# Attention-head operations of VectorE and ScalarE given a higher scheduling priority in a two-layer decoder trunk

## The chip, the cores and the metric

The kernel runs on one core of a Trainium2 chip. The metric is the device time in microseconds (us) of one execution. Lower is better.

The core has five engines that matter here. TensorE (PE in the profile) multiplies matrices; its weight loads are listed apart as PEld. VectorE is DVE, ScalarE is ACT, GpSimd is POOL, and SyncE (SP) issues the weight DMAs. Each engine has its own list of instructions, whose order is fixed when the program is built.

## The reference

A decoder trunk of two layers works on 256 tokens of width 2048, all in float32. Layer 0 normalises the tokens, projects them, and sends three quarters of the columns through a pooling mixer and one quarter through a 4-head attention over 256 memory rows. Layer 1 projects into queries for 12 differential heads and again 4 memory heads. Each layer ends in an output projection and a squared-ReLU MLP. What the change touches is the heads:

```python
# one differential head (layer 1), for two query/key maps
a = probs(q1b, k1) - lam * probs(q2b, k2)      # softmax of masked scores
o = jnp.einsum('bhqk,bkhd->bqhd', a, v)
token_out = rms_norm(o, subln_norm[b]) * (1.0 - lam_init)
# one memory head (both layers)
s = jnp.einsum('bqhd,bkhd->bhqk', q, k) * (MEM_HEAD_DIM ** -0.5)
o = jnp.einsum('bhqk,bkhd->bqhd', jax.nn.softmax(s, axis=-1), v)
```

## The kernel before, in words

**Weights.** All weights stream from one packed tensor `in_w` into SBUF as float32. TensorE works on a shorter float form, so each weight block is split in two: ScalarE rounds it into a high part (`hi_ring`, L157) and VectorE subtracts that from the original to get the low part (`lo_ring`, L158). A product is then high x high, high x low and low x high. This is the "making of high and low parts". Both parts live in a ring of six slots of 512 columns (`SLOTS`, L27). A unit of four 128-column blocks is called a quad here; it fills one slot. `Feed.fill` (L196) is called ahead of the matmuls of a quad and traces the splits up to three quads beyond it (`AHEAD`, L27). For some quads of the MLP's second matrix (the "slab" jobs) VectorE first forms sums of raw weights (L181 to L184).

**Projections.** `b_tile` (L423) computes a 256 x 512 tile in 16 steps of one quad and six matmuls (L417 to L419). `c_tile` (L400) computes 128 output columns in 16 blocks (L405 to L407). `a_part` (L377) does the same with a wide moving side (L391, L393). All of them call `tick()` once per quad.

**Heads.** The heads are woven between the quads. `at(d, fn)` (L280) puts a step of a head on a list, and `tick` (L283) traces it `d` quads later. A differential head (`diff_head`, L1175) has four steps. `scores` multiplies queries and keys on TensorE, adds the mask on VectorE (L1202, L1203; for heads 8 to 11 TensorE adds it), takes maxima (L1207), lets ScalarE exponentiate (L1211) and combines the two maps on VectorE (L1217 to L1221). `turn` transposes on TensorE (L1226) and copies on ScalarE (L1227). `pv` multiplies with the values (L1232 to L1234), takes squares on ScalarE (L1242) and scales on VectorE (L1250). `back` transposes (L1255) and writes high and low parts of the result into `cat1` (`split_gain`, L368). A memory head is `mem_query` (L541) and `mem_head` (L566), with the same kind of steps. `turn_queries` (L1155) transposes the queries and copies them on ScalarE (L1163). `query_rows`, `rope` and `query_scale` (L474 to L516) prepare the queries of four heads. The result tiles of all heads feed the output projection `out_tiles` (L1028), whose first three tiles need the last heads.

**What sets the order.** The program is traced in Python order, and each instruction's priority is its place in that order. When the program is built, a scheduler plays it through and puts, on each engine, the instruction with the best priority among those whose inputs and buffers it reckons to be ready. The result is a fixed list for each engine, which the chip runs in that order. In the kernel before, a step of a head that is traced at some tick stands ahead of the splits that are traced after that tick, and behind those traced before.

**Buffers around the change.** PSUM tiles: tag `s` (two), `t`, `o` and `st` (one each). SBUF tiles: tag `v` (six of 256 columns: `mq`, `mq_sq`, `osb`, `o_sq` and others), `m2` (twelve small columns).

Of the kernel before, what the change touches and what calls it, by code (L numbers as in the profile page):

```python
# [10 lines left out]
F32 = mybir.dt.float32  # L11
F32R = mybir.dt.float32r
BF16 = mybir.dt.bfloat16
AF = mybir.ActivationFunctionType
ALU = mybir.AluOpType
# [3 lines left out]
P = 128  # L19
# [243 lines left out]
def program(ctx, tc, plan, dry, xT, memT, par, lam, cst, wst, yT):  # L263
# [26 lines left out]
            tick()  # L290


    def vt(name):
        return tp.tile([P, T], F32, tag="v", bufs=6, name=name)

# [245 lines left out]
    def mem_query(src, gq, cols):  # L541


        q = vt("mq")
        sq = vt("mq_sq")
        nc.scalar.activation(q, src, AF.Copy, scale=gq)
        nc.scalar.activation(sq, src, AF.Square)
        y = tp.tile([P, 2], F32, tag="m2", bufs=12, name="mq_y")

        def stats():  # L550
            st = stat("st_mq")
            for t in range(2):
                nc.tensor.matmul(
                    st[:, 2 * t : 2 * t + 2], sq[:, t * P : t * P + P], ones_h,
                    start=True, stop=True,
                )
            v2 = tp.tile([P, 2], F32, tag="m2", bufs=12, name="mq_v")
            nc.vector.tensor_mul(v2, st[:, 0:4].rearrange("p (a b) -> p a b", b=2)[:, :, 0], cols[1])
            nc.vector.tensor_scalar_add(v2, v2, EPS)
            rsqrt_cols(y, v2)  # L560
            nc.vector.tensor_mul(y, y, cols[0])

        at(2, stats)
        return q, y

    def mem_head(q, y, k, v, e, pT, out, lag, pv_lag=6):  # L566

        def scores():  # L570
            s = pp.tile([P, 2, T], F32, tag="s", bufs=2, name="ms")
            for t in range(2):
                nc.tensor.matmul(s[:, t, :], q[:, t * P : t * P + P], k, start=True, stop=True)
            m = tp.tile([P, 2], F32, tag="m2", bufs=12, name="mm_max")
            nc.vector.tensor_reduce(out=m, in_=s, axis=AX.X, op=ALU.max, negate=True)
            nc.vector.tensor_mul(m, m, y)
            z = tp.tile([P, 2], F32, tag="m2", bufs=12, name="mm_sum")
            for t in range(2):
                nc.scalar.activation(
                    e[:, t, :], s[:, t, :], AF.Exp, bias=m[:, t : t + 1], scale=y[:, t : t + 1],  # L580
                    accum_out=z[:, t : t + 1],
                )
            zr = tp.tile([P, 2], F32, tag="m2", bufs=12, name="mm_rec")
            nc.vector.reciprocal(zr, z)
            for t in range(2):
                nc.vector.tensor_scalar_mul(e[:, t, :], e[:, t, :], zr[:, t : t + 1])

        def turn():
            t4 = pp.tile([P, 2, T], F32, tag="t", bufs=1, name="mt")
            for mb in range(2):  # L590
                for t in range(2):
                    nc.tensor.transpose(
                        t4[:, mb, t * P : t * P + P], e[:, t, mb * P : mb * P + P], ident
                    )
            nc.scalar.copy(pT, t4)

        def pv():
            o = pp.tile([P, T], F32, tag="o", bufs=1, name="mo")
            for mb in range(2):
                nc.tensor.matmul(o, v(mb), pT[:, mb, :], start=mb == 0, stop=mb == 1)  # L600
            nc.scalar.copy(out[:, 0:T], o)
            nc.vector.tensor_sub(out[:, T : 2 * T], o, out[:, 0:T].bitcast(F32))

        at(lag, scores)
        at(lag + 4, turn)
        at(lag + pv_lag, pv)
# [548 lines left out]
    def turn_queries(rows, i, pair):  # L1155
        t4 = pp.tile([P, 2, T], F32, tag="t", bufs=1, name="tq")
        for c in range(2):
            for t in range(2):
                nc.tensor.transpose(
                    t4[:, c, t * P : t * P + P], rows[:, t, (i + c) * P : (i + c) * P + P], ident  # L1160
                )
        for g, r in enumerate((slice(0, 64), slice(64, 128))):
            nc.scalar.activation(pair[g][r], t4[r], AF.Copy, scale=qcol[r])  # L1163


    gsub = cp.tile([P, 1], F32, name="gsub")
# [8 lines left out]
    def diff_head(h, q, y, lag, pv_lag, back_lag, by_pe):  # L1175
# [6 lines left out]
        def scores():  # L1182
            s1 = pp.tile([P, 2, T], F32, tag="s", bufs=2, name="s1")
            s0 = pp.tile([P, 2, P], F32, tag="s", bufs=2, name="s0")
            if by_pe:
                for m in range(2):
                    kk = kT[:, 6 * m + j, :]
                    nc.tensor.matmul(s1[:, m, :], q[:, m, P:T], kk, start=True, stop=False)
                    nc.tensor.matmul(s1[:, m, P:T], idb, mkb, start=False, stop=True)
                for m in range(2):  # L1190
                    kk = kT[:, 6 * m + j, 0:P]
                    nc.tensor.matmul(s0[:, m, :], q[:, m, 0:P], kk, start=True, stop=False)
                    nc.tensor.matmul(s0[:, m, :], idb, mkb, start=False, stop=True)
            else:
                for m in range(2):
                    kk = kT[:, 6 * m + j, :]
                    nc.tensor.matmul(s1[:, m, :], q[:, m, P:T], kk, start=True, stop=True)
                for m in range(2):
                    kk = kT[:, 6 * m + j, 0:P]
                    nc.tensor.matmul(s0[:, m, :], q[:, m, 0:P], kk, start=True, stop=True)  # L1200
                mask = const[:, C_MASK : C_MASK + P].unsqueeze(1).to_broadcast([P, 2, P])
                nc.vector.tensor_add(s1[:, :, P:T], s1[:, :, P:T], mask)  # L1202
                nc.vector.tensor_add(s0, s0, mask)  # L1203
            mx = tp.tile([P, 2, 2], F32, tag="m4", bufs=6, name="mx")
            z = tp.tile([P, 2, 2], F32, tag="m4", bufs=6, name="z")
            for t, s in ((1, s1), (0, s0)):
                nc.vector.tensor_reduce(out=mx[:, t, :], in_=s, axis=AX.X, op=ALU.max, negate=True)  # L1207
            nc.vector.tensor_mul(mx, mx, yh)
            for t, s, e in ((1, s1, e1), (0, s0, e0)):
                for m in range(2):  # L1210
                    nc.scalar.activation(  # L1211
                        e[:, m, :], s[:, m, :], AF.Exp, bias=mx[:, t, m : m + 1],
                        scale=yh[:, t, m : m + 1], accum_out=z[:, t, m : m + 1],
                    )

            zr = tp.tile([P, 2], F32, tag="m2", bufs=12, name="zr")
            nc.vector.reciprocal(zr, z[:, :, 1])  # L1217
            stt(zr, zr, nlam, z[:, :, 0], ALU.mult, ALU.mult)
            stt(ez, z[:, :, 0], EPS, z[:, :, 0], ALU.mult, ALU.mult)
            for t, e, dst in ((1, e1, a[:, P : P + T]), (0, e0, a[:, 0:P])):  # L1220
                stt(dst, e[:, 1, :], zr[:, t : t + 1], e[:, 0, :], ALU.mult, ALU.add)  # L1221

        def turn():
            t3 = pp.tile([P, 384], F32, tag="t", bufs=1, name="dt")
            for i in range(3):
                nc.tensor.transpose(t3[:, i * P : i * P + P], a[:, i * P : i * P + P], ident)  # L1226
            nc.scalar.copy(aT, t3)  # L1227

        def pv():
            o = pp.tile([P, 2, P], F32, tag="o", bufs=1, name="do")  # L1230
# [1 line left out]
            nc.tensor.matmul(o[:, 0, :], aT[:, 0:P], vv[:, 0, hs], start=True, stop=True)  # L1232
            nc.tensor.matmul(o[:, 1, :], aT[:, P:T], vv[:, 0, hs], start=True, stop=False)
            nc.tensor.matmul(o[:, 1, :], aT[:, T : T + P], vv[:, 1, hs], start=False, stop=True)  # L1234
            osb = vt("osb").rearrange("p (a b) -> p a b", a=2)
            if by_pe:
                nc.vector.tensor_copy(osb, o)
                o = osb
            ss = tp.tile([P, 2], F32, tag="m2", bufs=12, name="o_ss")
            junk = vt("o_sq")  # L1240
            for t in range(2):
                nc.scalar.activation(  # L1242
                    junk[:, t * P : t * P + P], o[:, t, :], AF.Square, accum_out=ss[:, t : t + 1]
                )
            v = tp.tile([P, 2], F32, tag="m2", bufs=12, name="o_v")
            stt(v, ss, 1.0 / P, ez, ALU.mult, ALU.add)
            yo = tp.tile([P, 2], F32, tag="m2", bufs=12, name="o_y")
            rsqrt_cols(yo, v)
            for t in range(2):
                nc.vector.tensor_scalar_mul(osb[:, t, :], o[:, t, :], yo[:, t : t + 1])  # L1250

            def back():
                f = pp.tile([P, T], F32, tag="st", bufs=1, name="o_t")
                for t in range(2):
                    nc.tensor.transpose(f[:, t * P : t * P + P], osb[:, t, :], ident)  # L1255
                split_gain(cat1[:, h, :], f, gsub)

            at(back_lag, back)

# [4 lines left out]
    for c in range(3):  # L1264
        ps = pair_of_banks(0, "q1")
        b_tile(ps, "w_in_q", 1, c, x_mx)
        rows, v = query_rows(ps, c1, 64)
        rope(rows, qtab)
        y = query_scale(v, c1)
        for i in range(2):  # L1270
            j = 2 * c + i
            q = qb[j % 3]
# [104 lines left out]
```

## Time and profile before

| what | value |
|---|---|
| median of 3 runs | 2045.28 us (2045.19 to 2045.52) |
| the profiled execution | 2044.93 us |
| its span, first to last instruction | 2043.1 us |
| granted TensorE clock | 1.000 of full speed |

How to read the profile. A row of the windows view gives, for a stretch in us from the start of the span, its length and then for each engine the busy time and the number of instructions, followed by the granted clock, the share of the DMA engines and the DMA rate. A row of the waits view names an engine and its instruction (by the tile that it writes and its line), what released it, and the total, the count and the longest of those waits. A row of the timeline gives start, duration, engine, line, operation, tiles written and read, shapes and a count; idle time just before it stands in square brackets. TensorE's matmuls overlap in the records: each is shown longer than the distance to the next one's start.

The heads of layer 0 run between about 60 and 130 us, those of layer 1 between about 1150 and 1280 us.

### The profile page before, as it was taken

Reading aid. Unit: us, or ns where it says so; the run is one execution under the profiler, and the core shown is the slowest. Engines: PE = TensorE matmul, PEld = TensorE weight load, DVE = VectorE, ACT = ScalarE, POOL = GpSimd, SP = SyncE. Lnnn points to the kernel's source line nnn. Section 1 sums busy time; section 2 is a strip of 40 time slices with the busy share of each in tenths; the row PEclk is TensorE's granted clock in tenths of the full one; section 3 lists DMA queues with packets and bytes.
Section 4 is the critical chain, followed back from the end, with each engine's and each line's share of the span. In section 5 each row is a group of like instructions: output and inputs, shape, how many; then the busy total and the mean of one; then the engine's idle time right before and its main releaser. Section 6 shows DMA issues by size and latency. Waiting matters only on the chain.

```text
span 2043.1 us, 32257 instructions
## 1 busy us (share of the span) xinstructions
PE 2037.2 (100%) x11060; PEld 1755.3 (86%) x11060; DVE 1716.2 (84%) x3215; ACT 1349.8 (66%) x2505; POOL 51.9 (3%) x67
## 2 busy tenths in 40 slices
PE   9999999999999999999999999999999999999999
PEld 8888888888888888888888888888888888888888
DVE  8888889889879978999766687889879978988997
ACT  7765566666666756768665697566657666666764
POOL 0001200000000000000000000310000000000000
PEclk9999999999999999999999999999999999999999
DMA  9556556555555555655565543656555555565564
GB/s 314 178 181 190 188 174 206 197 196 197 186 201 202 189 207 191 207 169 182 194 228 186 170 140 103 196 166 207 196 196 205 186 196 196 186 210 195 196 209 135
DMA packets 110470, 390.75 MB, mean 191 GB/s; under 512 B 12256, under 2 KB 14944, under 8 KB 110304
## 3 DMA queue, kind: packets, MB, share of 16 engines
q1 hardware_dynamic: 110160, 388.59, 57.1%
q8 instruction: 86, 1.41, 0.3%
q14 instruction: 80, 0.66, 0.1%
q10 hardware_dynamic: 144, 0.10, 0.0%
HBM read 386.54 MB, written 2.10 MB: 190 GB/s over the span
## 4 chain that ended last, share of the span: by engine, by line
PE 99%; ACT 1%; DVE 1%; issue 0%
PE x_bank L391 33%; PE x_bank L393 16%; PE wo L391 6%; PE p L746 5%; PE p L747 5%; PE p L748 5%; PE wo L393 3%; PE u L391 2%; PE ff L391 2%; PE u L393 1%; PE k L417 1%; PE k L419 1%; PE v L417 1%; PE k L418 1%; PE v L419 1%; PE v L418 1%
## 5 line engine op out<-in xcount | busy, mean ns | idle before, releaser
L157 ACT CAST hi_ring<-raw 128x512 fp32r<-128x512 f32 x1193 | 736.7, 620 | 529.5 <-PE x_bank L391 308.0
L158 DVE TENSOR_TENSOR lo_ring<-raw,hi_ring 128x512 fp32r<-128x512 f32 x1193 | 817.2, 695 | 206.7 <-ACT hi_ring L157 165.5
L391 PE MATMUL x_bank<-fx,hi_ring 128*128 128x512 f32 x1920 | 602.1, 395 | 0.0
L393 PEld LDWEIGHTS x_bank<-fx,lo_ring 128*128 128x128 f32 x1920 | 361.0, 188 | 83.6
L393 PE MATMUL x_bank<-fx,lo_ring 128*128 128x256 f32 x1920 | 377.4, 278 | 0.0
L391 PEld LDWEIGHTS x_bank<-fx,hi_ring 128*128 128x128 f32 x1920 | 301.4, 189 | 9.3
L391 PE MATMUL x_bank<-z,hi_ring 128*128 128x512 f32 x960 | 301.1, 395 | 0.0
L158 DVE TENSOR_TENSOR lo_ring<-slab,hi_ring 128x1024 fp32r<-128x1024 f32 x188 | 230.1, 1224 | 54.3 <-ACT hi_ring L157 53.6
L157 ACT CAST hi_ring<-slab 128x1024 fp32r<-128x1024 f32 x188 | 196.9, 1047 | 73.1 <-PE x_bank L391 36.2
L393 PEld LDWEIGHTS x_bank<-z,lo_ring 128*128 128x128 f32 x960 | 180.5, 188 | 41.7
L393 PE MATMUL x_bank<-z,lo_ring 128*128 128x256 f32 x960 | 188.8, 278 | 0.0
L391 PE MATMUL wo<-cat,hi_ring 128*128 128x512 f32 x512 | 162.5, 398 | 0.5 <-DVE resid L639 0.5
L391 PEld LDWEIGHTS x_bank<-z,hi_ring 128*128 128x128 f32 x960 | 151.9, 189 | 6.5 <-ACT room L672 0.4
L393 PEld LDWEIGHTS wo<-cat,lo_ring 128*128 128x128 f32 x512 | 95.9, 188 | 21.7
L672 ACT COPY room<-x_bank 128x512 f32<-128x512 f32 x180 | 104.9, 583 | 2.0 <-PE x_bank L393 2.0
L393 PE MATMUL wo<-cat,lo_ring 128*128 128x256 f32 x512 | 101.4, 279 | 0.0
L746 PE MATMUL p<-hi_ring,sit 128*128 128x512 f32 x256 | 100.5, 393 | 0.0
L747 PE MATMUL p<-hi_ring,sit 128*128 128x512 f32 x256 | 100.2, 391 | 0.0
L748 PE MATMUL p<-lo_ring,sit 128*128 128x512 f32 x256 | 99.7, 389 | 0.0
L391 PEld LDWEIGHTS wo<-cat,hi_ring 128*128 128x128 f32 x512 | 79.1, 189 | 2.2 <-PE wo L393 0.9
L717 ACT ACTIVATE room<-room 128x256 f32<-128x256 f32 x128 | 53.2, 416 | 39.1 <-DVE room L300 39.1
L746 PE MATMUL p<-hi_ring,z 128*128 128x512 f32 x192 | 75.2, 392 | 0.0
(313 smaller groups left out, 3102.3 us busy)
## 6 DMA issues: line engine op xcount, KB each, us to landing
raw<-in_w SPq DMA_DIRECT2D x595, 512.0 KB, 4.0
slab<-in_w SPq DMA_DIRECT2D x124, 512.0 KB, 3.3
resid<-in_x SPq DMA_DIRECT2D x8, 256.0 KB, 5.9
room<-in_w SPq DMA_DIRECT2D x4, 512.0 KB, 4.2
memraw<-in_mem SPq DMA_DIRECT2D x4, 512.0 KB, 3.6
out_y<-resid SPq DMA_DIRECT2D x16, 128.0 KB, 1.8
memraw<-in_mem SPq DMA_DIRECT2D x7, 256.0 KB, 6.3
raw<-in_w SPq DMA_DIRECT2D x3, 256.0 KB, 3.5
```

The source lines that it names most:

```text
L157: self.nc.scalar.copy(hi, src)
L158: self.nc.vector.tensor_sub(lo, src, hi.bitcast(F32))
L391: nc.tensor.matmul(ps, hi, xs[:, k, :], start=first and c == 0, stop=False)
L393: nc.tensor.matmul(ps[:, T : 2 * T], lo, xs[:, k, 0:T], start=False, stop=last and c == len(ks) - 1,)
L417: nc.tensor.matmul(ps[t], xl, hi, start=k == 0, stop=False)
L418: nc.tensor.matmul(ps[t], xh, hi, start=False, stop=False)
L419: nc.tensor.matmul(ps[t], xh, lo, start=False, stop=k == NK - 1)
L672: nc.scalar.copy(x, ps)
L717: at(3, lambda: nc.scalar.activation(stage[i % 8], y[:, 0:T], AF.Square))
L746: nc.tensor.matmul(ps, a[1], hi, start=first, stop=False)
L747: nc.tensor.matmul(ps, a[0], hi, start=False, stop=False)
L748: nc.tensor.matmul(ps, a[0], lo, start=False, stop=last)
```

## The change

A helper `early()` returns `tc.high_priority()`. Instructions traced inside it get the priority of the start of the program instead of their place in the order; after the block the count goes on as before. The VectorE and ScalarE operations of the heads are wrapped in it. No instruction is added or removed, and the matmuls, the transposes, the splits of the weights and the DMAs keep their priorities. The rest of the diff is indentation.

```diff
+    def early():
+
+        return tc.high_priority()
...
-        nc.scalar.activation(q, src, AF.Copy, scale=gq)
-        nc.scalar.activation(sq, src, AF.Square)
+        with early():
+            nc.scalar.activation(q, src, AF.Copy, scale=gq)
+            nc.scalar.activation(sq, src, AF.Square)
...
+            with early():
+                m = tp.tile([P, 2], F32, tag="m2", bufs=12, name="mm_max")
+                nc.vector.tensor_reduce(out=m, in_=s, axis=AX.X, op=ALU.max, negate=True)
...
-            nc.scalar.copy(pT, t4)
+            with early():
+                nc.scalar.copy(pT, t4)
...
+            with early():
+                nc.scalar.copy(out[:, 0:T], o)
+                nc.vector.tensor_sub(out[:, T : 2 * T], o, out[:, 0:T].bitcast(F32))
...
-            nc.scalar.activation(pair[g][r], t4[r], AF.Copy, scale=qcol[r])
+            with early():
+                nc.scalar.activation(pair[g][r], t4[r], AF.Copy, scale=qcol[r])
...
+                with early():
+                    nc.vector.tensor_add(s1[:, :, P:T], s1[:, :, P:T], mask)
+                    nc.vector.tensor_add(s0, s0, mask)
+            with early():
+                mx = tp.tile([P, 2, 2], F32, tag="m4", bufs=6, name="mx")
...
+            with early():
+                nc.scalar.copy(aT, t3)
...
+            with early():
+                osb = vt("osb").rearrange("p (a b) -> p a b", a=2)
...
+                with early():
+                    split_gain(cat1[:, h, :], f, gsub)
...
-        rows, v = query_rows(ps, c1, 64)
-        rope(rows, qtab)
-        y = query_scale(v, c1)
+        with early():
+            rows, v = query_rows(ps, c1, 64)
+            rope(rows, qtab)
+            y = query_scale(v, c1)
```

Inside the blocks lie: the query copies and squares and the statistics of `mem_query`; everything on VectorE and ScalarE in the `scores`, `turn` and `pv` steps of `mem_head`; the copies of `turn_queries`; and the mask, softmax, copy, norm and split operations of `diff_head`.

More of the change, by code (lines that the diff above doesn't have):

```diff
@@ L556, in stats @@
                 )
[L557 to L561, printed above, removed]
+            with early():
+                v2 = tp.tile([P, 2], F32, tag="m2", bufs=12, name="mq_v")
+                nc.vector.tensor_mul(v2, st[:, 0:4].rearrange("p (a b) -> p a b", b=2)[:, :, 0], cols[1])
+                nc.vector.tensor_scalar_add(v2, v2, EPS)
+                rsqrt_cols(y, v2)
+                nc.vector.tensor_mul(y, y, cols[0])
         at(2, stats)
@@ L573, in scores @@
                 nc.tensor.matmul(s[:, t, :], q[:, t * P : t * P + P], k, start=True, stop=True)
[L574 to L586, printed above, removed]
+            with early():
+                m = tp.tile([P, 2], F32, tag="m2", bufs=12, name="mm_max")
+                nc.vector.tensor_reduce(out=m, in_=s, axis=AX.X, op=ALU.max, negate=True)
+                nc.vector.tensor_mul(m, m, y)
+                z = tp.tile([P, 2], F32, tag="m2", bufs=12, name="mm_sum")
+                for t in range(2):
+                    nc.scalar.activation(
+                        e[:, t, :], s[:, t, :], AF.Exp, bias=m[:, t : t + 1], scale=y[:, t : t + 1],
+                        accum_out=z[:, t : t + 1],
+                    )
+                zr = tp.tile([P, 2], F32, tag="m2", bufs=12, name="mm_rec")
+                nc.vector.reciprocal(zr, z)
+                for t in range(2):
+                    nc.vector.tensor_scalar_mul(e[:, t, :], e[:, t, :], zr[:, t : t + 1])
         def turn():
@@ L600, in pv @@
                 nc.tensor.matmul(o, v(mb), pT[:, mb, :], start=mb == 0, stop=mb == 1)
-            nc.scalar.copy(out[:, 0:T], o)
-            nc.vector.tensor_sub(out[:, T : 2 * T], o, out[:, 0:T].bitcast(F32))
+            with early():
+                nc.scalar.copy(out[:, 0:T], o)
+                nc.vector.tensor_sub(out[:, T : 2 * T], o, out[:, 0:T].bitcast(F32))
         at(lag, scores)
@@ L1201, in scores @@
                 mask = const[:, C_MASK : C_MASK + P].unsqueeze(1).to_broadcast([P, 2, P])
[L1202 to L1218, printed above, removed]
@@ L1219, in scores @@
-            stt(ez, z[:, :, 0], EPS, z[:, :, 0], ALU.mult, ALU.mult)
-            for t, e, dst in ((1, e1, a[:, P : P + T]), (0, e0, a[:, 0:P])):
-                stt(dst, e[:, 1, :], zr[:, t : t + 1], e[:, 0, :], ALU.mult, ALU.add)
+                with early():
[3 more added lines that the diff above has]
+                mx = tp.tile([P, 2, 2], F32, tag="m4", bufs=6, name="mx")
+                z = tp.tile([P, 2, 2], F32, tag="m4", bufs=6, name="z")
+                for t, s in ((1, s1), (0, s0)):
+                    nc.vector.tensor_reduce(out=mx[:, t, :], in_=s, axis=AX.X, op=ALU.max, negate=True)
+                nc.vector.tensor_mul(mx, mx, yh)
+                for t, s, e in ((1, s1, e1), (0, s0, e0)):
+                    for m in range(2):
+                        nc.scalar.activation(
+                            e[:, m, :], s[:, m, :], AF.Exp, bias=mx[:, t, m : m + 1],
+                            scale=yh[:, t, m : m + 1], accum_out=z[:, t, m : m + 1],
+                        )
+                zr = tp.tile([P, 2], F32, tag="m2", bufs=12, name="zr")
+                nc.vector.reciprocal(zr, z[:, :, 1])
+                stt(zr, zr, nlam, z[:, :, 0], ALU.mult, ALU.mult)
+                stt(ez, z[:, :, 0], EPS, z[:, :, 0], ALU.mult, ALU.mult)
+                for t, e, dst in ((1, e1, a[:, P : P + T]), (0, e0, a[:, 0:P])):
+                    stt(dst, e[:, 1, :], zr[:, t : t + 1], e[:, 0, :], ALU.mult, ALU.add)
@@ L1226, in turn @@
                 nc.tensor.transpose(t3[:, i * P : i * P + P], a[:, i * P : i * P + P], ident)
-            nc.scalar.copy(aT, t3)
+            with early():
+                nc.scalar.copy(aT, t3)
         def pv():
@@ L1234, in pv @@
             nc.tensor.matmul(o[:, 1, :], aT[:, T : T + P], vv[:, 1, hs], start=False, stop=True)
[L1235 to L1250, printed above, removed]
+            with early():
+                osb = vt("osb").rearrange("p (a b) -> p a b", a=2)
+                if by_pe:
+                    nc.vector.tensor_copy(osb, o)
+                    o = osb
+                ss = tp.tile([P, 2], F32, tag="m2", bufs=12, name="o_ss")
+                junk = vt("o_sq")
+                for t in range(2):
+                    nc.scalar.activation(
+                        junk[:, t * P : t * P + P], o[:, t, :], AF.Square, accum_out=ss[:, t : t + 1]
+                    )
+                v = tp.tile([P, 2], F32, tag="m2", bufs=12, name="o_v")
+                stt(v, ss, 1.0 / P, ez, ALU.mult, ALU.add)
+                yo = tp.tile([P, 2], F32, tag="m2", bufs=12, name="o_y")
+                rsqrt_cols(yo, v)
+                for t in range(2):
+                    nc.vector.tensor_scalar_mul(osb[:, t, :], o[:, t, :], yo[:, t : t + 1])
             def back():
@@ L1255, in back @@
                     nc.tensor.transpose(f[:, t * P : t * P + P], osb[:, t, :], ident)
-                split_gain(cat1[:, h, :], f, gsub)
+                with early():
+                    split_gain(cat1[:, h, :], f, gsub)
             at(back_lag, back)
@@ L1266, in program @@
         b_tile(ps, "w_in_q", 1, c, x_mx)
-        rows, v = query_rows(ps, c1, 64)
-        rope(rows, qtab)
-        y = query_scale(v, c1)
+        with early():
+            rows, v = query_rows(ps, c1, 64)
+            rope(rows, qtab)
+            y = query_scale(v, c1)
         for i in range(2):
```

## The prediction

> **What bounds the kernel now.** I read the page's engine table and chain first, then windows of the two stages with heads, then the waits of TensorE's weight loads in them, then timelines of VectorE. The page:
>
> ```profile
> PE 2037.2 (100%) x11060; PEld 1755.3 (86%) x11060; DVE 1716.2 (84%) x3215; ACT 1349.8 (66%) x2505; POOL 51.9 (3%) x67
> ...
> PE 99%; ACT 1%; DVE 1%; issue 0%
> ```
>
> TensorE is busy for 2037.2 of 2043.1 us, and 99% of the chain that ended last is its own work. No other engine can gain anything except by ending a wait of TensorE. So the question is how much TensorE waits in the two stages that the change touches, and the windows answer it:
>
> ```profile
> 60.00:130.00 70.00, 70.00 (x395) 60.20 (x394) 59.12 (x129) 47.74 (x103) 0.00 (x0) 1.00 0.58 177
> ...
> 1150.00:1280.00 130.00, 128.56 (x802) 113.23 (x801) 106.49 (x352) 104.33 (x317) 1.67 (x3) 1.00 0.39 127
> ```
>
> In layer 0's stage TensorE has no gap at all (70.00 of 70.00), and its weight loads wait for no step of a memory head there. In layer 1's it is idle for 130.00 - 128.56 = 1.44 us. That is a floor, because a matmul is shown longer than the distance to the next one's start and covers the beginning of a gap. The weight loads show more of each wait. Their waits in the same window, all of them:
>
> ```profile
> PEld mt L592 <- DVE att L586: 1.2, 2, 1.0
> PEld tq L1159 <- ACT att L1163: 0.8, 2, 0.5
> PEld dt L1226 <- ACT att L1163: 0.5, 2, 0.4
> PEld wo L391 <- PE wo L393: 0.5, 1, 0.5
> PEld dt L1226 <- ACT hi_ring L157: 0.3, 1, 0.3
> PEld o_t L1255 <- DVE osb L1250: 0.2, 1, 0.2
> PEld wo L391 <- DVE cat L602: 0.2, 1, 0.2
> PEld wo L391 <- DVE cat L300: 0.2, 1, 0.2
> PEld mo L600 <- ACT att L595: 0.2, 1, 0.2
> ```
>
> Everything but `wo <- PE wo` waits for a step of a head: 1.2 + 0.8 + 0.5 + 0.3 + 0.2 + 0.2 + 0.2 + 0.2 = 3.6 us. The reader should see two things. First, no row names `lo_ring`, and one alone names `hi_ring`, ahead of a transpose: TensorE never waits here for a weight. Second, 3.6 us is 0.18% of 2045. If every wait for a head vanished, the kernel would gain less than 0.2%, which is about what a measurement of this kernel can tell from no change.
>
> [...]
>
> **The change part by part.** It adds and removes no instruction and no DMA; it moves VectorE's and ScalarE's head operations ahead of the splits in those engines' lists. How much is moved past how much? The splits' own rows, for the same two windows:
>
> ```profile
> 1150.00:1280.00 130.00, 79.66 (x296) 49.73 (x296) 37.73 (x56) 34.79 (x58) 1.00 0.39 127
> ```
>
> These are the instructions that touch `hi_ring`: 37.73 us on VectorE and 34.79 on ScalarE. What is left, 106.49 - 37.73 = 68.8 us of VectorE and 104.33 - 34.79 = 69.5 of ScalarE, is mostly heads: about 68.8 / 16 = 4.3 us of VectorE for each of the 16 heads.
>
> *What goes first already.* A split is ready when TensorE frees its slot, six quads ahead, but it is traced only three quads ahead. A head step that is due is therefore traced before a split that is four or five quads early, and has the better priority even now. Only when the ring has run down to three quads do splits come first. VectorE's timeline shows just that:
>
> ```profile
> 1205.97 0.68 DVE L158 TENSOR_TENSOR lo_ring<-raw,hi_ring 128x512 fp32r<-128x512 f32 x1
> ...
> 1208.03 0.16 DVE L300 SCALAR_TENSOR_TENSOR ez<-z 128x2 f32<-128x2 f32 x1 [0.91 <-ACT att L1211]
> ...
> 1214.18 0.70 DVE L158 TENSOR_TENSOR lo_ring<-raw,hi_ring 128x512 fp32r<-128x512 f32 x1
> ...
> 1215.28 0.17 DVE L362 TENSOR_TENSOR rc<-rc,o_v 128x2 f32<-128x2 f32 x1
> 1215.35 0.70 DVE L158 TENSOR_TENSOR lo_ring<-raw,hi_ring 128x512 fp32r<-128x512 f32 x1
> 1215.95 0.17 DVE L300 SCALAR_TENSOR_TENSOR o_y<-rc 128x2 f32<-128x2 f32 x1
> 1216.02 0.70 DVE L158 TENSOR_TENSOR lo_ring<-raw,hi_ring 128x512 fp32r<-128x512 f32 x1
> ```
>
> For 8.2 us, from 1205.97 to 1214.18, VectorE makes no low part and runs heads and queries. Then splits and head operations alternate, and there the head operation behind a split needed the one just before it: `o_y` reads what L362 began to write at 1215.28 and needs 0.17 us for, so at 1215.35 it was not ready. A scheduler that starts whatever is ready takes the split there under either priority. So the change should move little. Cost of this part: between 0 and the 3.6 us above as a gain; I take 0, except in one place.
>
> *The one place.* The longest wait, 1.0 us, is that of the third memory head's transpose `mt`, near 1261 us. VectorE before it:
>
> ```profile
> 1257.32 0.15 DVE L361 TENSOR_TENSOR rc<-rc 128x2 f32<-128x2 f32 x1
> 1257.39 0.68 DVE L182 TENSOR_TENSOR room<-slab,slab 128x512 f32<-128x512 f32 x1
> 1257.99 0.15 DVE L362 TENSOR_TENSOR rc<-rc,mq_v 128x2 f32<-128x2 f32 x1
> 1258.11 0.69 DVE L183 TENSOR_TENSOR slab<-room,slab 128x512 f32<-128x512 f32 x1
> 1258.71 0.15 DVE L300 SCALAR_TENSOR_TENSOR mq_y<-rc 128x2 f32<-128x2 f32 x1
> 1258.79 0.69 DVE L575 TENSOR_REDUCE mm_max<-ms 128x2 f32<-128x512 f32 x1
> ```
>
> Two slab sums (L182, L183) stand between the small operations of that head and put it back by (1257.99 - 1257.39) + (1258.71 - 1258.11) = 1.2 us. If the scheduler holds VectorE's next small operation as ready at once, priority removes both and the whole 1.2 us of `mt` waits with them. If it reckons with the 0.15 us that each needs, the sums go in as before and nothing is gained; the maximum L575, which could run in between, points to the first. Between 0 and 1.2 I take the middle, 0.6 us.
>
> *What is put back.* Splits and slab sums, by one to three operations of 0.15 to 0.69 us each. The cover is the ring. ScalarE's waits in the window show how full it is:
>
> ```profile
> ACT hi_ring L157 <- PE q L418: 7.8, 9, 2.0
> ACT hi_ring L157 <- PE wo L391: 5.0, 8, 1.0
> ACT hi_ring L157 <- PE mq L406: 3.7, 5, 1.5
> ```
>
> ScalarE stands 16.5 us, 22 times, with nothing to do but a split whose slot TensorE has not freed: all six slots are full then. The tightest place is the low part that began at 1214.18 and was ready at 1214.88. Counting the quads, its first reader is this matmul:
>
> ```profile
> 1216.71 0.28 PE L407 MATMUL mq<-x_mx,lo_ring 128*128 128x256 f32 x1
> ```
>
> The cover there is 1.83 us. Without it each further 0.1 us costs TensorE 0.1 us. I take this cost as 0, with a far end in the rivals. After the `mt` wait, `wo <- PE wo` (0.5 us, a bank that the residual's addition frees) is late next; no head operation bears on it, so it stays.
>
> **The sum.** 2044.93 (the profiled execution: 2043.1 of span and 1.83 around it) - 0.6 + 0 = 2044.3. That execution lay 0.35 us under the median of its kernel, so the median of the changed kernel should be 2044.3 + 0.35 = **2044.7 us**.
>
> **The rivals.**
>
> *The ring runs dry (slower).* Head operations of two heads follow each other on VectorE without a gap, and the protection that the old order gave at three quads is gone. Place: the stretch from 1205.97 to 1216.71. Condition: more than 1.83 us of head work ready at 1214.18. Price: with one more head's 4.3 us in front, the low part is ready at 1214.88 + 4.3 = 1219.2, and TensorE waits 2.5 us at 1216.71. VectorE and ScalarE have hardly room to make up for it:
>
> ```profile
> 1130.00:1140.00 10.00, 10.00 (x46) 8.29 (x45) 5.33 (x8) 4.35 (x7) 0.00 (x0) 1.00 0.57 185
> ...
> 1210.00:1220.00 10.00, 9.95 (x81) 9.49 (x80) 9.74 (x37) 9.48 (x29) 0.00 (x0) 1.00 0.26 73
> ```
>
> At 1210 to 1220 VectorE is busy for 9.74 of 10 us. The queries come in three groups, so such a place can come once to three times: 2.5 to 7.5 us, 2047.8 to 2052.8, and 2050.3 for two. For it: those busy shares. Against it: head operations wait for each other (the 0.91 us gap at 1208.03), and each such gap lets a split in. [...]
>
> *All waits go (faster).* The head steps come early enough that all 3.6 us vanish, and the 0.5 us of `wo <- PE wo` with them because the last head ends sooner: 2045.28 - 4.1 = 2041.2. For it: the waits are all just in time. Against it: the argument above that heads go first already. A smaller relative of it is that TensorE has room of its own, weight loads running for only 113.23 of 130 us, which would allow 16.8 us, 2028.5. The row from 1130 to 1140 speaks against that: there TensorE does nothing but `b_tile`, no wait shows, and the loads still take 8.29 of 10. So 83% is what a full TensorE shows, and the head stage's 87% is full as well. [...]
>
> *The lists hardly change, or are shuffled (neither).* If heads go first already, the change does not do what it says. The scheduler may also put transposes and scores into other places between the quads. At 2045.3 the lists are the same; a few waits come or go in a shuffle, up to half of the 3.6 us either way: 2043.5 to 2047.1.
>
> **How the numbers follow.** Forecast (gain of 0 to 3.6 us, nothing starves): 0.45, its own range 2041.7 to 2045.3. Shuffled or unchanged: 0.20. Ring dry: 0.26, of which I give 0.24 to more than 4.1 us (0.2%) and 0.02 to less. All waits and the bank's: 0.09, of which 0.01 for room of TensorE's own and 0.01 for a time just inside 0.2%. So faster 0.08, within 0.2% 0.45 + 0.20 + 0.02 + 0.01 = 0.68, slower 0.24. The range reaches from 2041.2 up to 2050.3, the price of two dry places, and leaves out some 0.12 above and 0.05 below.
>
> **What would show it.** Right: in the changed profile the weight loads' waits between 1150 and 1280 us come to 2 to 4 us, none names `lo_ring`, and L182 and L183 no longer stand between L361 and L575. The slow rival: rows `PE` or `PEld <- DVE lo_ring L158` (or `<- ACT hi_ring`) of 2 us and more, near the ends of the query groups. The fast one: TensorE without a gap from 1150 to 1280. No change: ScalarE's 16.5 us of waits for slots stay within a few tenths. The forecast is wrong if the scheduler, once heads come first, lets them pile up so that the ring is empty when they are done.

## The result and the profile after

| kernel | median, us | lowest to highest | ratio to the kernel before, 95% interval |
|---|---|---|---|
| before | 2045.28 | 2044.79 to 2046.08 (9 runs) | |
| after | 2051.95 | 2049.71 to 2053.28 (9 runs) | 1.0031 [1.0021, 1.0042] |

The change made the kernel slower by 6.7 us. The profiled execution of after took 2052.62 us with a span of 2050.8, against 2043.1. Line numbers move with the diff: transposes of a memory head are L599 (L592 before), its maximum L582 and L583 (L575 and L576), the output projection L395 and L397 (L391 and L393), the scalar-and-tensor operation L304 (L300), the differential head's transposes L1238 and L1269 (L1226 and L1255). The splits keep L157 and L158, the slab sums L182 and L183.

The windows of after, for the two stages with heads (length, then busy time of PE, PEld, DVE, ACT and POOL, granted clock, DMA share and rate):

```profile
60.00:130.00 70.00, 70.00 (x394) 60.15 (x393) 59.09 (x128) 47.86 (x103) 0.00 (x0) 1.00 0.55 179
1150.00:1280.00 130.00, 125.70 (x767) 109.70 (x766) 100.71 (x342) 100.80 (x309) 0.00 (x0) 0.97 0.36 116
```

Layer 0 is as full as it was. In layer 1's stage TensorE is idle for 4.30 us instead of 1.44, and a second thing is new: the granted clock is 0.97. Slices of 5 us, first of before, then of after, show where it lies:

```profile
1260.00:1265.00 5.00, 4.24 (x26) 3.58 (x25) 3.71 (x16) 4.47 (x20) 0.00 (x0) 1.00 0.30 105
1265.00:1270.00 5.00, 5.00 (x30) 4.28 (x29) 4.58 (x17) 3.37 (x9) 0.00 (x0) 1.00 0.29 105
```

```profile
1260.00:1265.00 5.00, 2.27 (x13) 1.50 (x11) 3.69 (x13) 2.79 (x10) 0.00 (x0) 0.96 0.33 105
1265.00:1270.00 5.00, 4.95 (x17) 4.40 (x18) 1.88 (x9) 2.50 (x12) 0.00 (x0) 0.50 0.00 0
1270.00:1275.00 5.00, 4.62 (x22) 3.67 (x21) 2.92 (x11) 2.57 (x7) 0.00 (x0) 0.85 0.31 105
```

From 1260 to 1265 TensorE works 2.27 of 5 us; from 1265 to 1270 it is busy, but with 17 instructions instead of 30, because its granted clock there is 0.50. The waits of its weight loads between 1150 and 1280 us in after, all rows:

```profile
PEld mt L599 <- DVE att L593: 2.2, 1, 2.2
PEld wo L395 <- DVE cat L304: 2.0, 2, 1.2
PEld o_t L1269 <- issue: 1.0, 2, 0.9
PEld dt L1238 <- ACT att L1173: 0.9, 2, 0.5
PEld tq L1168 <- ACT att L1173: 0.7, 2, 0.5
PEld do L1245 <- ACT att L1240: 0.4, 1, 0.4
PEld dt L1238 <- issue: 0.3, 2, 0.2
PEld dt L1238 <- ACT hi_ring L157: 0.3, 1, 0.3
PEld mo L608 <- issue: 0.3, 1, 0.3
PEld s L1202 <- ACT att L586: 0.3, 1, 0.3
```

They come to 8.4 us, against 4.1 for all rows before. Of these 1.6 us stand in rows with `issue`, which name no releaser; the rows that name a step of a head come to 6.5 us, against 3.3. Again no row names `lo_ring`, and the one with `hi_ring` is 0.3 us as before: TensorE still does not wait for weights. It waits for heads, which the change was to hurry. VectorE's timeline shows where they lose the time. First before, then after, at the third differential head (start, duration, engine, line, operation, tiles):

```profile
1174.97 0.22 DVE L300 SCALAR_TENSOR_TENSOR zr<-zr,nlam,z 128x2 f32<-128x2 f32 x1
1175.23 0.75 DVE L300 SCALAR_TENSOR_TENSOR att<-att,zr 128x256 f32<-128x256 f32 x2
```

```profile
1176.88 0.22 DVE L304 SCALAR_TENSOR_TENSOR zr<-zr,nlam,z 128x2 f32<-128x2 f32 x1
1177.01 0.69 DVE L158 TENSOR_TENSOR lo_ring<-raw,hi_ring 128x512 fp32r<-128x512 f32 x1
1177.62 0.43 DVE L1213 TENSOR_TENSOR s<-s,const 128x256 f32<-128x256 f32 x1
1177.95 0.42 DVE L1214 TENSOR_TENSOR s<-s,const 128x256 f32<-128x256 f32 x1
1178.28 1.01 DVE L1219 TENSOR_REDUCE mx<-s 128x2 f32<-128x512 f32 x2
1179.21 0.48 DVE L304 SCALAR_TENSOR_TENSOR cat<-o_t,gsub,cat 128x256 fp32r<-128x256 f32 x1
...
1179.74 0.74 DVE L304 SCALAR_TENSOR_TENSOR att<-att,zr 128x256 f32<-128x256 f32 x2
```

Before, the last step of the head's scores (`att`) began 0.26 us after `zr`. After, it began 2.86 us after it, behind the masks and maxima of the next head, traced later, and the result of another. The reason is in the diff. Each block inside `early()` starts at the program's start and counts up from there. `att` holds the 11th and 12th places of a `scores` block; the masks and the maximum hold the first places of theirs. So the first operations of any later head now outrank the last operations of an earlier one. Among themselves the heads have lost the order in which they were traced. Here other matmuls cover the loss: TensorE began the projection for the first memory head at 1206.60 us, against 1206.35, and it had been 0.4 us later than before already at 1150. By the end of the stage it had even run ahead with the weights, because late steps of heads left their places to weight matmuls; the first matmul of the output projection, before and after:

```profile
1251.53 0.81 PE L391 MATMUL wo<-cat,hi_ring 128*128 128x512 f32 x2
```

```profile
1248.85 0.63 PE L395 MATMUL wo<-cat,hi_ring 128*128 128x512 f32 x2
```

So the weight matmuls that could have covered the last heads were used up 2.7 us earlier. VectorE of after there, with the operations of memory heads two, three and four:

```profile
1247.47 0.69 DVE L158 TENSOR_TENSOR lo_ring<-raw,hi_ring 128x512 fp32r<-128x512 f32 x1 [0.23 <-ACT hi_ring L157]
1248.08 0.15 DVE L583 TENSOR_TENSOR mm_max<-mm_max,mq_y 128x2 f32<-128x2 f32 x1
...
1262.41 0.69 DVE L158 TENSOR_TENSOR lo_ring<-raw,hi_ring 128x512 fp32r<-128x512 f32 x1
1263.02 0.15 DVE L583 TENSOR_TENSOR mm_max<-mm_max,mq_y 128x2 f32<-128x2 f32 x1
...
1271.44 0.69 DVE L158 TENSOR_TENSOR lo_ring<-raw,hi_ring 128x512 fp32r<-128x512 f32 x1 [2.27 <-ACT hi_ring L157]
...
1273.09 0.15 DVE L564 TENSOR_TENSOR mq_v<-st_mq,d_x 128x2 f32<-128x2 f32 x1
...
1281.97 0.42 DVE L611 TENSOR_TENSOR cat<-mo,cat 128x256 fp32r<-128x256 f32 x1 [1.05 <-ACT cat L610]
```

The same four steps of before:

```profile
1245.53 0.15 DVE L576 TENSOR_TENSOR mm_max<-mm_max,mq_y 128x2 f32<-128x2 f32 x1
...
1259.85 0.15 DVE L576 TENSOR_TENSOR mm_max<-mm_max,mq_y 128x2 f32<-128x2 f32 x1
...
1265.24 0.15 DVE L558 TENSOR_TENSOR mq_v<-st_mq,d_x 128x2 f32<-128x2 f32 x1
...
1274.45 0.42 DVE L602 TENSOR_TENSOR cat<-mo,cat 128x256 fp32r<-128x256 f32 x1 [1.13 <-ACT cat L601]
```

Second head 2.6 us late, third 3.2, fourth 7.9, and the last result 7.5 us late; 0.4 us of each was there before the stage. TensorE is idle on the way for the results of two differential heads (`cat`, 0.76 and 0.38 us) and for the third memory head's transposes (2.03 us). In the new lists a split stands ahead of the head's own next step, the reverse of what the change is for. VectorE took its list in order here: at 1271.44 the split had stopped it for 2.27 us, and `mq_v` stood behind the split and began at 1273.09, though TensorE had finished its input `st_mq` at 1267.02. The split's high part was late on ScalarE, which waited for a ring slot that TensorE, at a clock of 0.50, had not freed:

```profile
1266.17 0.85 PE L558 MATMUL st_mq<-ones_h,mq_sq 128*128 128x2 f32 x4
...
1270.79 0.62 ACT L157 CAST hi_ring<-raw 128x512 fp32r<-128x512 f32 x1 [1.38 <-PE wo L395]
```

### The profile page after: what moved, and what is told of

It reads as the page before. It is cut to its first block, busy times and chain, and to the rows that moved or that the text cites. A ratio compares the mean times of both kernels' runs of the same rounds, so it can differ in the third digit from the quotient of the medians.

```text
span 2050.8 us, 32262 instructions
## 1 busy us (share of the span) xinstructions
PE 2040.5 (99%) x11060; PEld 1755.7 (86%) x11060; DVE 1715.8 (84%) x3215; ACT 1350.1 (66%) x2505; POOL 51.9 (3%) x67
## 4 chain that ended last, share of the span: by engine, by line
PE 98%; ACT 1%; DVE 1%; DMA 0%; issue 0%; SPq 0%; DVEq 0%
PE x_bank L395 33%; PE x_bank L397 16%; PE wo L395 6%; PE p L755 5%; PE p L756 5%; PE p L757 5%; PE wo L397 3%; PE u L395 2%; PE ff L395 2%; PE u L397 1%; PE k L421 1%; PE k L423 1%; PE v L422 1%; PE v L423 1%; PE k L422 1%; PE v L421 1%
## 5 line engine op out<-in xcount | busy, mean ns | idle before, releaser
L157 ACT CAST hi_ring<-raw 128x512 fp32r<-128x512 f32 x1193 | 736.4, 620 | 530.2 <-PE x_bank L395 304.1
L158 DVE TENSOR_TENSOR lo_ring<-raw,hi_ring 128x512 fp32r<-128x512 f32 x1193 | 817.8, 695 | 211.2 <-ACT hi_ring L157 166.4
L395 PE MATMUL x_bank<-fx,hi_ring 128*128 128x512 f32 x1920 | 601.8, 395 | 0.0
L397 PEld LDWEIGHTS x_bank<-fx,lo_ring 128*128 128x128 f32 x1920 | 360.6, 188 | 84.0
L397 PE MATMUL x_bank<-fx,lo_ring 128*128 128x256 f32 x1920 | 377.1, 278 | 0.0
L395 PEld LDWEIGHTS x_bank<-fx,hi_ring 128*128 128x128 f32 x1920 | 301.3, 189 | 9.4
L395 PE MATMUL x_bank<-z,hi_ring 128*128 128x512 f32 x960 | 300.9, 395 | 0.0
L158 DVE TENSOR_TENSOR lo_ring<-slab,hi_ring 128x1024 fp32r<-128x1024 f32 x188 | 230.2, 1224 | 54.3 <-ACT hi_ring L157 53.5
L157 ACT CAST hi_ring<-slab 128x1024 fp32r<-128x1024 f32 x188 | 196.8, 1047 | 73.1 <-PE x_bank L395 37.5
L397 PEld LDWEIGHTS x_bank<-z,lo_ring 128*128 128x128 f32 x960 | 180.3, 188 | 41.9
L397 PE MATMUL x_bank<-z,lo_ring 128*128 128x256 f32 x960 | 188.6, 278 | 0.0
L395 PE MATMUL wo<-cat,hi_ring 128*128 128x512 f32 x512 | 163.6, 400 | 2.1 <-DVE cat L304 1.1
L395 PEld LDWEIGHTS x_bank<-z,hi_ring 128*128 128x128 f32 x960 | 151.8, 189 | 6.4 <-ACT room L681 0.4
L397 PEld LDWEIGHTS wo<-cat,lo_ring 128*128 128x128 f32 x512 | 96.5, 189 | 21.8
L397 PE MATMUL wo<-cat,lo_ring 128*128 128x256 f32 x512 | 102.8, 281 | 0.0
L395 PEld LDWEIGHTS wo<-cat,hi_ring 128*128 128x128 f32 x512 | 79.4, 190 | 4.4 <-DVE cat L304 2.4
```

Source lines behind the costliest of these rows:

```text
L157: self.nc.scalar.copy(hi, src)
L158: self.nc.vector.tensor_sub(lo, src, hi.bitcast(F32))
L395: nc.tensor.matmul(ps, hi, xs[:, k, :], start=first and c == 0, stop=False)
L397: nc.tensor.matmul(ps[:, T : 2 * T], lo, xs[:, k, 0:T], start=False, stop=last and c == len(ks) - 1,)
```

## The experiments

| run | what of the change it has | median, us | ratio, 95% interval | clock of its profile |
|---|---|---|---|---|
| e1_mem_only | memory heads only | 2046.83 | 1.0006 [0.9997, 1.0014] | 1.000 |
| e2_diff_only | differential heads and queries only | 2048.32 | 1.0014 [1.0005, 1.0023] | 0.998 |
| e3_own_after | all, last memory head with a buffer of its own | 2050.22 | 1.0022 [1.0013, 1.0031] | 0.999 |
| e4_own_before | none, the same buffer | 2044.70 | 0.9997 [0.9988, 1.0006] | 1.000 |
| e5_offset | all, but 200 places up | 2045.72 | 1.0001 [0.9992, 1.0009] | 1.000 |
| e6_first | all but the last heads | 2046.84 | 1.0007 [0.9998, 1.0016] | 1.000 |
| e7_last | the last heads only | 2051.55 | 1.0029 [1.0017, 1.0040] | 0.998 |
| e8_warm | all, four idle-time matmuls added | 2049.87 | 1.0021 [1.0012, 1.0030] | 1.000 |
| e9_offset_own | e5 and e3 together | 2044.87 | 0.9999 [0.9990, 1.0007] | 1.000 |
| e10_offset_pe | e5, TensorE's head steps too | 2046.41 | 1.0004 [0.9995, 1.0013] | 1.000 |

Runs e1 to e4 stand against 2045.60 us of the kernel before, e5 to e8 against 2045.54, e9 and e10 against 2045.33. Each median is of eleven executions, that of e7_last of six. The last column is of one execution, the profiled one.

### Buffers, or the order of the lists? (e1 to e4)

The first three theories were: A, the last memory head's query has to wait for a buffer of tag `v`, which heads that go first hold; B, the order of the lists itself; C, the lower clock.

e1_mem_only takes the priority from every block of the differential heads and their queries, of which one is shown; `late()` returns an empty `ExitStack()`, which sets no priority. e2_diff_only does it the other way round:

```diff
-            with early():
+            with late():
                 nc.scalar.activation(pair[g][r], t4[r], AF.Copy, scale=qcol[r])
```

> Only the operations of the memory heads keep the high priority; those of the differential heads and their queries have their old place. Theory A (the six buffers of tag v are handed out in another order, and the differential heads take them from the last memory heads): the memory heads now come first, the last of them ends as in the kernel before or earlier, 2043 to 2046 us. Theory B (the order of the lists as such, whichever heads go first, puts small waits in a row): between the two kernels, 2047 to 2050 us.

> The other half: only the differential heads, their queries and the copies of the turned queries keep the high priority. Theory A: the whole loss or more, 2050 to 2054 us. Theory B: between the two kernels, 2047 to 2050 us.

e3_own_after (on after) and e4_own_before (on before), for the fourth memory head of layer 1:

```diff
-        q = vt("mq")
-        sq = vt("mq_sq")
+        if own:
+            both = tp.tile([P, 512], F32, tag="rowsq", bufs=1, name="mq_own")
+            q, sq = both[:, 0:T], both[:, T : 2 * T]
+        else:
+            q, sq = vt("mq"), vt("mq_sq")
```

> The changed kernel, in which the query copy and its squares of the last memory head have a buffer of their own (the tile of tag rowsq, unused at that time) and take none of the six of tag v. Theory A: the last memory head starts about ten us earlier and most of the 6.7 us go, 2043 to 2047 us. Theory B: the loss stays, 2050 to 2053 us. Theory C (a good part of the loss is TensorE's granted clock, which fell to 0.5 near 1265 us after a gap): wherever the gaps before 1265 us shrink under 2 us the clock stays at 1.000 and some 2 to 3 us go with it.

> The kernel before with the same buffer for its last memory head. Theory A: the tail is bound by these buffers there too, so the 1 to 2 us of waits near 1261 and 1277 us shrink, 2043 to 2045 us. Theory B: no change, 2045.0 to 2045.6 us.

The buffer gave back about 1.7 us of after (2051.95 to 2050.22) and nothing measurable of before, so A falls as the main cause. The differential heads alone cost 2.7 us and the memory heads alone 1.2, an amount whose interval still reaches to no change; both together cost 6.7, more than the sum. That fits B in kind, but not throughout: e1's 2046.83 us lies between the times given for A and for B, and e4's 2044.70 within those for A. Nor does B say yet what in the order does it. C is open: e2 has the low clock and e1 has not. Its condition, no gap of 2 us, does not hold: in e3 the longest idle gap of TensorE before the fall was 1.17 us, and the clock still was 0.81 from 1270 to 1275 us.

### Ahead of the splits, or out of order among themselves? (e5)

This run tells apart the two things that the change does at once. Theory D is the loss of order among the heads, described above.

```diff
     def early():
 
-        return tc.high_priority()
+        return tc.high_priority(offset=200)
```

> The whole change, but its operations move up by 200 places instead of to the start of the program. They still stand ahead of every high and low part made near them, and among themselves they keep the order in which they were traced. Theory B (it is the place ahead of the high and low parts that hurts: VectorE and ScalarE run heads just in time and splits end up in front of the last heads): 2049 to 2052 us, with the same 2 us wait of TensorE near 1263 us. Theory D (it is the order among the heads that hurts: each wrapped block counts from the start of the program, so the first operations of a later head overtake the last operations of an earlier one): 2043.5 to 2046.5 us, granted clock 1.000, slab sums L182 and L183 behind the maximum of the third memory head.

With 200 places every head operation still outranks the splits traced near it, and the heads keep their order. The 6.7 us are gone: 1.0001 [0.9992, 1.0009]. D stands and B, as worded there, falls: to go ahead of the splits costs nothing that can be measured. (An order against instructions traced more than 200 places earlier is changed back by this run as well; nothing in the traces points to one.) VectorE of this run at the third differential head, at the slab sums and at the end:

```profile
1175.86 0.22 DVE L304 SCALAR_TENSOR_TENSOR zr<-zr,nlam,z 128x2 f32<-128x2 f32 x1
1176.11 0.75 DVE L304 SCALAR_TENSOR_TENSOR att<-att,zr 128x256 f32<-128x256 f32 x2
...
1259.64 0.15 DVE L583 TENSOR_TENSOR mm_max<-mm_max,mq_y 128x2 f32<-128x2 f32 x1
1259.70 0.69 DVE L182 TENSOR_TENSOR room<-slab,slab 128x512 f32<-128x512 f32 x1
...
1275.34 0.42 DVE L611 TENSOR_TENSOR cat<-mo,cat 128x256 fp32r<-128x256 f32 x1 [1.25 <-ACT cat L610]
```

`att` follows `zr` at 0.25 us again, the third memory head's maximum is done before the slab sum, and the last result comes at 1275.34. How a lost order among heads brings a split ahead of a head's next step is only argued: the scheduler plays the program through, and where an earlier step of that head came late in its play, the split was ready and the step was not. But e5 is no gain either. These are waits of TensorE's weight loads for the last heads between 1150 and 1280 us in it:

```profile
...
PEld mt L599 <- DVE att L593: 0.7, 2, 0.5
...
PEld o_t L1269 <- DVE mq_v L564: 0.6, 2, 0.4
PEld wo L395 <- DVE cat L304: 0.5, 1, 0.5
```

The wait for `mt` fell from 1.2 to 0.7 us, and `o_t` (0.6) and `wo <- cat` (0.5) are late instead.

### Where in the stage? (e6, e7)

```diff
-        with early():
+        go = early if c < 2 else late
+        with go():
             rows, v = query_rows(ps, c1, 64)
...
+        go = early if h < 2 else late
```

This is e6_first; e7_last has `c == 2` (the differential heads and their queries) and `h >= 2` (the memory heads).

> The change for the first eight differential heads, their queries and the first two memory heads of layer 1 only; the last four differential heads and the last two memory heads as before. Theory that only the tail sets the time (in the stretch before 1240 us TensorE has enough other matmuls to cover a late head): 2045 to 2047 us. Rival (lateness gathered in the earlier heads carries into the tail): 2049 to 2052 us.

> The change for the last four differential heads, their queries and the last two memory heads of layer 1 only; the rest of layer 1 as before. Theory that only the tail sets the time: 2049 to 2052 us. Rival (lateness gathered in the earlier heads carries into the tail): 2045 to 2047 us.

The last heads alone carry nearly all of the loss: 2051.55 against 2051.95 for the whole change. The first ten heads of layer 1 cost 1.3 us, an amount whose interval still reaches to no change. In e6's trace TensorE is idle for 0.71 and 0.70 us near 1262, where it was idle once for 0.76 before, so that what the first heads cost also falls at the last ones. (Layer 0's memory heads have the change in both runs.) The window of e7_last from 1265 us shows the half clock of after:

```profile
1265.00:1270.00 5.00, 3.91 (x14) 3.34 (x14) 2.25 (x10) 3.32 (x15) 0.00 (x0) 0.50 0.00 0
```

### What the clock costs (e8)

```diff
             t4 = pp.tile([P, 2, T], F32, tag="t", bufs=1, name="mt")
+            for _ in range(warm):
+                nc.tensor.matmul(t4[0:2, 0, :], mmax[0], q, start=True, stop=True)
```

`warm` is 4 in the third memory head of layer 1 and 0 elsewhere.

> The changed kernel with four more matmuls of TensorE, into the bank of the third memory head's transposes just ahead of them; the transposes overwrite what they write. They fill the idle time near 1263 us and all other instructions stand in the order of the changed kernel. Theory C (TensorE's idle time near 1263 us lowers the granted clock, and the 6 us at 0.50 after it are about half of the loss): granted clock 1.000, 2048 to 2050 us. If the clock costs nothing that the waits of the tail do not take anyway: 2051 to 2052.5 us with the clock at 1.000.

On TensorE the added matmuls (L601, which the profile lists as eight) lie in the idle time, and the transposes (L604) begin at 1265.15 us as against 1265.05 in after; e8's rows begin about 0.1 us later throughout:

```profile
1263.32 1.89 PE L601 MATMUL mt<-mq,mm_max 128*2 128x256 f32 x8 [0.20 <-DVE mm_max L586]
1265.15 0.33 PE L604 MATMUL mt<-const,att 128*128 128x128 f32 x1
```

```profile
1260.00:1265.00 5.00, 4.03 (x21) 2.10 (x19) 3.69 (x13) 2.70 (x9) 0.00 (x0) 1.00 0.33 105
1265.00:1270.00 5.00, 5.00 (x30) 4.39 (x30) 3.03 (x14) 3.77 (x15) 0.00 (x0) 1.00 0.00 0
```

The clock stays at 1.00, 30 instructions run from 1265 to 1270 instead of 17, and the kernel takes 2049.87 us. So C is a part of the loss, 2.1 us of the median, and not "about half" as it was put. The one run of after whose mean clock was 1.000 says the same: it took 2049.71 us, the lowest of the nine. Six of the others had 0.999 and two 0.998. The profiled one is of the two, 2.8 us above e8, so its trace shows more of the low clock than the median run had. What is left, 4.3 us over the kernel before, goes with the late heads: e5, without them, does not have it. (4.3 and 2.1 are 6.4 and not 6.7 because the kernel before took 2045.54 us beside e8 and 2045.28 beside after.)

### Two versions that might have beaten both (e9, e10)

e9_offset_own puts e5's and e3's edits together. e10_offset_pe wraps each head step with its matmuls, at 200 places; `inside` keeps the blocks within a step from moving up twice:

```diff
+    def at_head(d, fn):
+
+        def go():
+            with early():
+                inside[0] = True
+                fn()
+                inside[0] = False
+
+        at(d, go)
+
...
+        return ExitStack() if inside[0] else tc.high_priority(offset=200)
...
-        at(lag, scores)
+        at_head(lag, scores)
```

> The 200-place priority with a buffer of their own for the copy and the square of the last memory head's query, so that they need not wait for a buffer of the common tag. If buffers still hold the last head back where the order is right: 2043.5 to 2045, below the kernel before. If the tail's waits only move to the next step, as the 200-place priority alone showed: 2045 to 2046.5, no difference that can be measured.

> The 200-place priority for the matmuls and transposes of the heads as well, so that TensorE's list has each head step ahead of the weight matmuls traced near it. If the heads are late because their steps on TensorE stand behind weight matmuls: 2043.5 to 2045. If a head step that goes first on TensorE makes TensorE wait for it instead: 2046 to 2050 with more waits of PE for att and cat between 1150 and 1290 us.

Neither beats the kernel before by anything that can be measured. e9's 2044.87 us lies inside the first expectation, but its interval holds 1. e10's median lies inside the second one's times, but not by what it named: the weight loads' waits for `att` and `cat` between 1150 and 1290 us come to 2.8 us, against 3.1 before. So why e10 is 1.1 us up stays open, if it is.

## Why the prediction was wrong

- **What bounds the kernel.** TensorE does, and the 3.6 us of waits (0.3 of them in the row with `hi_ring`) were not exceeded by any gain: e5, e9 and e4 move nothing that can be measured. But waits in a trace of before bound a gain and not a loss. On the losing side the prediction had only the ring, and a shuffle of at most 1.8 us.
- **What goes first already: this step failed.** It asked only how heads stand to splits, found that a due head step goes ahead even now, and concluded that the change "should move little", cost 0. For heads and splits that holds: e5 does that alone, and its ratio is 1.0001. But the change does a second thing, stated in the section on the change: a block gets the priority of the program's start, not a place some way up. That puts heads in another order among themselves, and it cost the 6.7 us: 2051.95 with that order, 2045.72 without. The step should have asked for every pair that the new priority compares: head with split, and head with head.
- **The one place.** In after L182 and L183 still stand between the head's small operations and its maximum (1259.96 and 1260.67 us on VectorE, the maximum L582 at 1261.75), so the 0.6 us could not come. With the order kept, e5, the mechanism was right: L182 went behind the maximum, and the wait for `mt` fell by 0.5 us. But the next waits took it over, and the time shows no gain.
- **What is put back.** Right. No wait names `lo_ring`, and layer 0's stage has no gap.
- **The rivals.** *The ring runs dry* gave 2047.8 to 2052.8, which holds the measured time, but by a mechanism that did not occur: the loss lies at 1260 to 1285, not at 1206 to 1217, and in heads, not in weights. *The lists are shuffled* was the right kind of event. Its size, half of today's waits either way, was wrong: a shuffled list can add waits that do not exist yet. It added 4.3 us of waits and 2.1 us of clock.
- **The clock.** The sum has no term for a lower clock, and every row of before that it rests on has 1.00. In after's profile the clock was 0.50 from 1265 to 1270 us; e8, in whose profile it stayed at 1.00, is 2.1 us below after in the median.
- **Why only the tail counts** was not asked at all. The last heads end in `wo` matmuls that need their results, and TensorE had taken up the weight matmuls beside them 2.7 us sooner; behind a late head little was left. At 1177 us a head 2.6 us late cost nothing: TensorE was no later at 1206.60 than at 1150.

## What to carry to other kernels

When a change gives a group of operations "high priority", compare the new priorities within the group as well: a priority that starts again in every block reverses the order of a chain's last steps and a later chain's first. A bounded step up keeps the order, and it shows whether going first is worth anything before the rest is disturbed. Look for the cost where a chain has nothing beside it, at the end of a stage; waits seen there today limit what can be gained, not what can be lost.

## What the runs showed of the hardware

In the profile of after TensorE's granted clock was 0.50 from 1265 to 1270 us. Ahead of that TensorE was idle for 0.76 us, then worked for about 1.2 us, and was idle again for 2.03:

```profile
1261.82 0.50 PE L395 MATMUL wo<-cat,hi_ring 128*128 128x512 f32 x1 [0.76 <-DVE cat L304]
...
1265.05 0.47 PE L599 MATMUL mt<-const,att 128*128 128x128 f32 x1 [2.03 <-DVE att L593]
```

Estimated from the windows above, read as a mix of 1.00 and 0.50, the fall lies near 1264.6 us (0.96 over 5 us is 0.4 us at 0.50) and the return near 1271.5 (0.85 is 1.5 us): about 6.9 us at 0.50. By that estimate the fall came inside the second gap, when TensorE had been idle for 0.76 us and then for about 1.6. In e2_diff_only TensorE had a single gap, of 2.03 us, between 1258 us and the fall (near 1263.7 us, from 0.87 between 1260 and 1265); its row and the window behind it:

```profile
1263.71 1.16 PE L603 MATMUL mt<-const,att 128*128 128x128 f32 x4 [2.03 <-DVE att L597]
```

```profile
1265.00:1270.00 5.00, 5.00 (x17) 4.25 (x17) 1.95 (x12) 1.98 (x8) 0.00 (x0) 0.50 0.00 0
```

In e7_last the clock fell near 1264.0 us (0.90 from 1260 to 1265) after gaps of 0.71 and 0.89 us, and in e3_own_after near 1273.1 (0.81 from 1270 to 1275, 0.85 in the next 5 us), for about 3.4 us only, after gaps of 1.17 and 1.09. e6_first had gaps of 0.71 and 0.70 us and kept 1.00 in its profile. The program alone does not decide: after, unchanged, ran at a mean clock of 1.000 once in nine runs, and e7_last twice in six. What decides is not shown.
